# Holding the accumulation of f's leftover row behind the low part of its piece, in an encoder layer in split fp32

## The chip, the cores and the metric

The kernel runs on one core of one Trainium2 chip. The metric is the device time of one execution in microseconds (us), taken as the median of several runs. Besides that there is one execution recorded by the hardware profiler; its span runs from the first to the last instruction on the core.

## The reference

One encoder layer on x, 256 tokens of 2048 channels, all float32: a feed-forward half-step, a mixer, a second feed-forward half-step. The mixer is what matters here:

```python
u = _rms_norm(h, pre_g)
q, k, v, f, g = jnp.split(u @ w_in, SPLIT_POINTS, axis=-1)
q = _apply_axial_rope(_rms_norm(q.reshape(b, s, N_Q_HEADS, HEAD_DIM), q_norm_g), rope)
k = _apply_axial_rope(_rms_norm(k.reshape(b, s, N_KV_HEADS, HEAD_DIM), k_norm_g), rope)
...
y_attn = _blocked_gqa(q, k, v) @ w_attn_o
y_four = _fourier_mix(f) @ w_fourier
...
merged = gates[:, :, 0] * y_attn + gates[:, :, 1] * y_four
return h + _rms_norm(merged @ w_out, post_g)
```

`_fourier_mix` splits f (1024 channels) into 8 groups of 128 channels and takes the real part of the two-dimensional FFT over the 256 positions and the 128 channels of a group. g gives the gates through a sigmoid.

## The kernel before

**Numbers and pieces.** Every matrix product is done with fp32 values split in two: a high part (ScalarE copies the value into the matmul's reduced format, L101) and a low part (VectorE subtracts the high part from the value, L102). `split` does both and notes the two instructions as `latest["A"]` and `latest["V"]`. `mm3` makes three matmuls of one product: high by high (L106), weight's low (L107), activation's low (L108). A weight piece is 512 KB: two contraction rows of 128 by 512 columns (`piece`, L112). It is loaded by SyncE (L82) into one of 5 buffers `raw`, and its parts go into a ring of 6 high and 6 low buffers (`wring`), which become free when TensorE has used them.

**The stages.** First feed-forward (11 blocks of 512 hidden columns), then the mixer, then the second feed-forward. In the mixer a column block (`col_block`, L187) makes 512 columns of u @ w_in for both halves of the tokens: 16 contraction rows, 2 token tiles and 3 matmuls, 96 matmuls of 512 columns, with 8 weight pieces. `between` and `at` are lists of other work that is put among its matmuls. The order of the mixer around the change (L844 to L859) is v; gate 10, with the folding of the tokens and norm and rope of k among it; q's first block; gate 11, with norm and rope of q among it; gate 12, with the transposes of k; gate 13; then attention, with the Fourier parts among its first gate.

**The projection to f.** f is not made like q or k. The tokens come mirrored, so `fold_tokens` (L566) makes the even sum and the odd difference of the two token tiles, transposes them and splits them (`ueo`). The column of the transposed odd tile that has no partner is kept in `o0`, one value for each of the 2048 channels. The weight of f comes as 16 pieces, one for each contraction row, 512 KB each: `load_f` (L615) loads a piece into a buffer `fraw` (SyncE, L618) and then lets GpSimd's queue add the mirrored columns on the way from memory (252 KB, L613). The buffers come from the pool `chunk`, two tags of 3 buffers each, and pieces alternate between the tags: 6 buffers.

`fold_f` (L622) does one piece. It starts the load of the piece four further on, forms the differences of the mirrored columns on VectorE (L631, in place, held behind the latest low part by `tc.issue_after`), splits the piece (L101, L102), and adds 12 matmuls of 260 or 252 columns (names pe, accumulators `pfold`). Then follows the leftover row: z2, 128 x 520, gets the piece's first 260 columns of both halves times o0's value of this row, summed over the 16 pieces on VectorE (L642 for piece 0, L644 for the others; the profile names the tile zs). After the last piece `pfold` is split (fs), and `fourier_positions` (L660) reads zs and fs. `folds_at(4)` spreads four folds over a column block, one behind each of its rows 1, 5, 9 and 13: folds 0 to 3 lie in q's first block, 4 to 7 in gate 11, 8 to 11 in gate 12, 12 to 15 in gate 13.

**What sets the order.** Each engine works through its instructions in order. The order is made when the program is built: a scheduler places each instruction on its engine's queue by when its inputs, its buffers and its engine are free in the scheduler's plan, with the program's order as preference. So an instruction without further ties may stand well ahead of its place in the program. `with tc.issue_after(ins):` adds to every instruction in the block that runs on `ins`'s engine the tie that it comes after `ins` in that queue; it is no wait on another engine. One stretch (L303) is under a manual schedule for VectorE; the folds are not.

Of the kernel before, what the change touches and what calls it, by code (L numbers as in the profile page):

```python
# [15 lines left out]
ALU = mybir.AluOpType  # L16
# [38 lines left out]
def encoder_layer(  # L55
# [23 lines left out]
    V, A, T = nc.vector, nc.scalar, nc.tensor  # L79
# [18 lines left out]
    latest = {}  # L98

    def split(hi, lo, src):  # L100
        a = A.activation(hi, src, AF.Copy)  # L101
        v = V.tensor_tensor(out=lo, in0=src, in1=hi.bitcast(F32), op=ALU.subtract)  # L102
        latest["A"], latest["V"] = a.ins, v.ins

    def mm3(ps, lh, ll, rh, rl, first, last):
        T.matmul(ps, lh, rh, start=first, stop=False)  # L106
        T.matmul(ps, lh, rl, start=False, stop=False)  # L107
        return T.matmul(ps, ll, rh, start=False, stop=last)  # L108
# [415 lines left out]
    for nm, g in (("q", gq), ("k", gk)):  # L524
        gc = const.tile([P, NT, HD], F32, name="gc" + nm)
        gs = const.tile([P, NT, HD], F32, name="gs" + nm)
        for t in range(NT):
            V.tensor_tensor(out=gc[:, t, :], in0=rc[:, t, :], in1=g[:], op=ALU.mult)
            v = lambda a: a.rearrange("p (a h c) -> p a h c", a=2, h=2)
            for half in range(2):  # L530
                V.tensor_tensor(out=v(gs[:, t, :])[:, :, half, :], in0=v(rsn[:, t, :])[:, :, half, :],
                                in1=v(g[:])[:, :, 1 - half, :], op=ALU.mult)
# [30 lines left out]
    o0 = const.tile([P, KD], F32, name="o0")  # L563
# [44 lines left out]
    z2 = xpool.tile([P, 2, EW], F32, tag="xt", name="zs")  # L608
# [6 lines left out]
    def load_f(k):  # L615
        raw = chunk.tile([P, 2, NB], F32, tag=("ch_hi", "ch_lo")[k % 2], name="fraw")
        src = w_f[k].rearrange("p (b c) -> p b c", b=2)
        load(raw[:], src)  # L618
        add_on_the_way(raw[:, :, 0:OW], src[:, :, EW:NB])
        fraw[k] = raw  # L620

    def fold_f(k):  # L622

        if k == 0:
            pfold[0] = pmm.tile([P, NB], F32, tag="mm", name="pe")
            pfold[1] = ptr.tile([P, NB], F32, tag="tr", name="pe")
        if k + F_AHEAD < KD:
            load_f(k + F_AHEAD)
        raw = fraw.pop(k)
        with tc.issue_after(latest["V"]):  # L630
            V.scalar_tensor_tensor(out=raw[:, :, EW:NB], in0=raw[:, :, EW:NB], scalar=-2.0, in1=raw[:, :, 0:OW],  # L631
                                   op0=ALU.mult, op1=ALU.add)
        hi = wring.tile([P, 2, NB], F32R, tag="hi", name="whi")
        lo = wring.tile([P, 2, NB], F32R, tag="lo", name="wlo")
        split(hi[:], lo[:], raw[:])
        e, o = slice(0, EW), slice(EW, NB)
        for b in range(2):
            mm = mm3(pfold[b][:, e], ueo[0][0][:, k, :], ueo[0][1][:, k, :], hi[:, b, e], lo[:, b, e], k == 0, False)
            with tc.issue_after(mm.ins):
                mm3(pfold[b][:, o], ueo[1][0][:, k, :], ueo[1][1][:, k, :], hi[:, b, o], lo[:, b, o], False, k == KD - 1)  # L640
        if k == 0:
            V.tensor_scalar(out=z2[:], in0=raw[:, :, e], scalar1=o0[:, k:k + 1], scalar2=None, op0=ALU.mult)  # L642
        else:
            V.scalar_tensor_tensor(out=z2[:], in0=raw[:, :, e], scalar=o0[:, k:k + 1], in1=z2[:],  # L644
                                   op0=ALU.mult, op1=ALU.add)
        if k == KD - 1:
            fs.extend(chunk.tile([P, 2, NB], F32R, tag="ch_" + c, name="f" + c[0]) for c in ("hi", "lo"))
            for b in range(2):
                split(fs[0][:, b, :], fs[1][:, b, :], pfold[b][:])
# [3 lines left out]
    def folds_at(n):  # L653

        now = [folds.pop(0) for _ in range(n)]
        return [(1 + i * KD // n, lambda k=k: fold_f(k)) for i, k in enumerate(now)]
# [389 lines left out]
```

## Time and profile before

| | us |
|---|---|
| Median of 3 runs | 2110.78 (2110.67 to 2111.9) |
| The profiled execution | 2111.38 |
| Its span | 2109.6 |
| Mean granted TensorE clock | 0.992 of full speed |

How to read the lines that follow: a group or timeline line has the source line, the engine (PE is TensorE, PEld its weight loads, DVE VectorE, ACT ScalarE, POOL GpSimd, SP SyncE), the operation, and out<-in by the program's names. In a timeline the first two numbers are the start and the duration in us, and the bracket holds how long the engine had been idle and what ended that. A row of a stretch gives its length, then busy us with the number of instructions in brackets for PE, PEld, DVE, ACT and POOL, then the granted clock, the busy share of the DMA engines, and GB/s. A waits line reads: who, for whom, us in total, times, the longest. A matmul's own duration is longer than the distance to the next one, since matmuls are pipelined.

### The profile page before, as it was taken

What the parts mean: (1) busy time and instruction counts of PE and PEld (TensorE: products, weight loads), DVE (VectorE), ACT (ScalarE), POOL (GpSimd) and SP (SyncE); (2) the same over time, 40 slices, a digit from 0 to 9 for tenths busy, and PEclk for the clock granted to TensorE, in tenths of its full rate; (3) what the DMA queues carried; (4) which work ended last, traced back from release to release, by engine and by line L of the source; (5) the groups of instructions that cost most, each with busy time, mean ns of one, the idle gap of its engine ahead of it and who ended that gap; (6) DMA issues with size and microseconds to landing.
All of it is one profiled execution on the core that took longest, in us unless ns stands there. A gap on an engine that the chain in (4) does not pass through costs nothing.

```text
span 2109.6 us, 25216 instructions
## 1 busy us (share of the span) xinstructions
PE 2065.4 (98%) x9466; PEld 1711.0 (81%) x9466; DVE 1317.7 (62%) x1682; ACT 1008.5 (48%) x1336; POOL 50.8 (2%) x46
## 2 busy tenths in 40 slices
PE   9999999999999998799999999999999999999998
PEld 7888888888888877678888888878888888888886
DVE  6545555555555787567877886874555555555556
ACT  7444444444444555345676464554444444444443
POOL 0000000000000110100000000200000000000001
PEclk9999999999999999899999999999999999999999
DMA  8665655655655695664555657466555556555663
GB/s 317 221 214 191 189 191 189 193 191 189 191 189 196 204 286 175 166 180 156 182 178 180 209 174 265 163 195 212 191 191 190 190 191 195 190 189 189 192 191 108
DMA packets 117868, 411.11 MB, mean 195 GB/s; under 512 B 12873, under 2 KB 19025, under 8 KB 116337
## 3 DMA queue, kind: packets, MB, share of 16 engines
q1 hardware_dynamic: 113392, 405.36, 58.8%
q0 software_dynamic: 4352, 4.13, 1.3%
q8 instruction: 74, 1.21, 0.2%
q14 instruction: 50, 0.40, 0.1%
HBM read 405.25 MB, written 4.19 MB: 194 GB/s over the span
## 4 chain that ended last, share of the span: by engine, by line
PE 53%; DVE 3%; DMA 2%; issue 1%; ACT 0%; DVEq 0%; POOLq 0%; ACTq 0%
PE pc L106 10%; PE pc L108 10%; PE pc L107 10%; PE pr L108 6%; PE pr L107 6%; PE pr L106 6%; DMA fraw<-in_w_f 1%; DVE wlo L102 1%; PE pt L177 1%; DMA raw<-in_w_fo 1%; PE pt L761 0%; PE pf L108 0%; PE pf L106 0%; PE pf L107 0%; DVE h L390 0%
## 5 line engine op out<-in xcount | busy, mean ns | idle before, releaser
L102 DVE TENSOR_TENSOR wlo<-raw,whi 128x1024 fp32r<-128x1024 f32 (+1 forms) x711 | 866.4, 1221 | 669.6 <-ACT whi L101 668.0
L101 ACT ACTIVATE whi<-raw 128x1024 fp32r<-128x1024 f32 (+1 forms) x711 | 751.3, 1059 | 872.1 <-PE pc L108 525.0
L106 PE MATMUL pc<-whi,uh 128*128 128x512 f32 x1840 | 721.9, 392 | 1.5 <-ACT uh L485 1.5
L107 PE MATMUL pc<-wlo,uh 128*128 128x512 f32 x1840 | 719.6, 391 | 2.0 <-DVE wlo L102 2.0
L108 PE MATMUL pc<-whi,ul 128*128 128x512 f32 x1840 | 719.1, 391 | 2.0 <-DVE ul L102 2.0
L108 PEld LDWEIGHTS pc<-whi,ul 128*128 128x128 f32 x1840 | 347.0, 189 | 75.0 <-DVE ul L102 3.0
L106 PEld LDWEIGHTS pc<-whi,uh 128*128 128x128 f32 x1840 | 347.1, 189 | 73.8 <-ACT uh L485 3.3
L107 PEld LDWEIGHTS pc<-wlo,uh 128*128 128x128 f32 x1840 | 347.1, 189 | 73.8 <-DVE wlo L102 3.9
L106 PE MATMUL pr<-whi,hTh 128*128 128x512 f32 x688 | 269.5, 392 | 0.0
L108 PE MATMUL pr<-whi,hTl 128*128 128x512 f32 x688 | 267.9, 389 | 0.0
L107 PE MATMUL pr<-wlo,hTh 128*128 128x512 f32 x688 | 267.9, 389 | 0.0
L108 PEld LDWEIGHTS pr<-whi,hTl 128*128 128x128 f32 x688 | 129.2, 188 | 26.8
L106 PEld LDWEIGHTS pr<-whi,hTh 128*128 128x128 f32 x688 | 129.2, 188 | 26.1
L107 PEld LDWEIGHTS pr<-wlo,hTh 128*128 128x128 f32 x688 | 129.3, 188 | 26.0
L219 DVE TENSOR_TENSOR yf<-pr,yf 128x512 f32<-128x512 f32 (+1 forms) x82 | 55.1, 673 | 10.4 <-PE pr L108 9.7
L219 DVE TENSOR_TENSOR y<-pr,y 128x512 f32<-128x512 f32 x80 | 54.7, 685 | 4.5 <-PE pr L108 4.0
L106 PE MATMUL pr<-whi,oTh 128*128 128x512 f32 x128 | 50.3, 393 | 0.0
L108 PE MATMUL pr<-whi,oTl 128*128 128x512 f32 x128 | 50.0, 390 | 0.0
L107 PE MATMUL pr<-wlo,oTh 128*128 128x512 f32 x128 | 49.9, 390 | 0.0
L106 PE MATMUL pr<-whi,mTh 128*128 128x512 f32 x120 | 46.9, 391 | 0.0
L108 PE MATMUL pr<-whi,mTl 128*128 128x512 f32 x120 | 46.7, 389 | 0.0
L107 PE MATMUL pr<-wlo,mTh 128*128 128x512 f32 x120 | 46.7, 389 | 0.0
(300 smaller groups left out, 1378.0 us busy)
## 6 DMA issues: line engine op xcount, KB each, us to landing
raw<-in_f_up SPq DMA_DIRECT2D x176, 512.0 KB, 4.6
raw<-in_f_down SPq DMA_DIRECT2D x176, 512.0 KB, 4.5
raw<-in_f_gate SPq DMA_DIRECT2D x175, 512.0 KB, 4.4
raw<-in_w_in SPq DMA_DIRECT2D x112, 512.0 KB, 4.8
raw<-in_w_ao SPq DMA_DIRECT2D x32, 512.0 KB, 3.8
raw<-in_w_out SPq DMA_DIRECT2D x32, 512.0 KB, 4.2
fraw<-in_w_f SPq DMA_DIRECT2D x16, 512.0 KB, 6.0
raw<-in_w_fo SPq DMA_DIRECT2D x16, 512.0 KB, 4.3
```

The costliest lines, as they stand in the source:

```text
L101: a = A.activation(hi, src, AF.Copy)
L102: v = V.tensor_tensor(out=lo, in0=src, in1=hi.bitcast(F32), op=ALU.subtract)
L106: T.matmul(ps, lh, rh, start=first, stop=False)
L107: T.matmul(ps, lh, rl, start=False, stop=False)
L108: return T.matmul(ps, ll, rh, start=False, stop=last)
L177: T.transpose(pt[:, j, :], src[:, j * P:(j + 1) * P], ident[:])
L219: V.tensor_tensor(out=dst, in0=ps, in1=dst, op=ALU.add)
```

## The change

The two instructions that accumulate the leftover row are put under `tc.issue_after(latest["V"])`. At that place `latest["V"]` is the low part of the same piece, made by the `split` a few lines earlier. What is computed, and in which sums, stays as it was.

```diff
@@ -638,11 +638,12 @@
-        if k == 0:
-            V.tensor_scalar(out=z2[:], in0=raw[:, :, e], scalar1=o0[:, k:k + 1], scalar2=None, op0=ALU.mult)
-        else:
-            V.scalar_tensor_tensor(out=z2[:], in0=raw[:, :, e], scalar=o0[:, k:k + 1], in1=z2[:],
-                                   op0=ALU.mult, op1=ALU.add)
+        with tc.issue_after(latest["V"]):
+            if k == 0:
+                V.tensor_scalar(out=z2[:], in0=raw[:, :, e], scalar1=o0[:, k:k + 1], scalar2=None, op0=ALU.mult)
+            else:
+                V.scalar_tensor_tensor(out=z2[:], in0=raw[:, :, e], scalar=o0[:, k:k + 1], in1=z2[:],
+                                       op0=ALU.mult, op1=ALU.add)
```

## The prediction

> **What bounds the kernel now.** The page comes first: TensorE is busy nearly throughout, so the change can only pay where TensorE stands still. The two --windows rows below it (busy time in a stretch) compare all of the folding of f with its last part.
>
> ```profile
> PE 2065.4 (98%) x9466; PEld 1711.0 (81%) x9466; DVE 1317.7 (62%) x1682; ACT 1008.5 (48%) x1336; POOL 50.8 (2%) x46
> ```
> ```profile
> 814.97:955.23 140.26, 116.28 (x549) 97.65 (x548) 84.01 (x122) 58.52 (x83) 10.01 (x10) 0.90 0.60 172
> 927.71:955.23 27.52, 27.52 (x145) 23.65 (x144) 19.39 (x21) 14.65 (x15) 0.00 (x0) 1.00 0.56 182
> ```
>
> The stretch runs from fold 0's first matmul to fold 15's. TensorE works 116.28 of 140.26 us there, at a granted clock of 0.90. From fold 11 to fold 15 it works all of 27.52 us at clock 1.00: four cycles, so one cycle (four rows of a column block and one fold) takes 6.88 us when nothing is missing. Who TensorE waits for, and who VectorE waits for, is in the waits of 725 to 960 us (total, times, longest):
>
> ```profile
> PE pe L107 <- DVE wlo L102: 16.0, 6, 6.1
> PE pe L106 <- ACT q L546: 6.3, 1, 6.3
> PE pe L106 <- ACT whi L101: 1.6, 2, 1.2
> ```
> ```profile
> DVE zs L644 <- DMA fraw<-in_w_f: 36.4, 7, 7.1
> DVE zs L644 <- issue: 4.2, 1, 4.2
> ```
>
> TensorE lacks mostly the low part of a piece of f (16.0 us), which VectorE writes. VectorE itself stands 36.4 + 4.2 = 40.6 us in front of the accumulation of the leftover row, zs at L644, for a piece that has not landed. VectorE's timeline shows which piece:
>
> ```profile
> 820.49 0.76 DVE L644 SCALAR_TENSOR_TENSOR zs<-fraw,o,zs 128x520 f32<-128x520 f32 x1 [4.56 <-DMA fraw<-in_w_f]
> ...
> 854.00 2.35 DVE L102 TENSOR_TENSOR wlo<-raw,whi 128x1024 fp32r<-128x1024 f32 x2
> 856.27 0.68 DVE L631 SCALAR_TENSOR_TENSOR fraw<-fraw 128x504 f32<-128x504 f32 x1
> 864.03 0.76 DVE L644 SCALAR_TENSOR_TENSOR zs<-fraw,o,zs 128x520 f32<-128x520 f32 x1 [7.09 <-DMA fraw<-in_w_f]
> 864.71 1.22 DVE L102 TENSOR_TENSOR wlo<-fraw,whi 128x1024 fp32r<-128x1024 f32 x1
> ...
> 888.58 0.76 DVE L644 SCALAR_TENSOR_TENSOR zs<-fraw,o,zs 128x520 f32<-128x520 f32 x1 [5.74 <-DMA fraw<-in_w_f]
> 889.26 1.22 DVE L102 TENSOR_TENSOR wlo<-fraw,whi 128x1024 fp32r<-128x1024 f32 x1
> ...
> 937.89 2.35 DVE L102 TENSOR_TENSOR wlo<-raw,whi 128x1024 fp32r<-128x1024 f32 x2
> 940.16 0.67 DVE L631 SCALAR_TENSOR_TENSOR fraw<-fraw 128x504 f32<-128x504 f32 x1
> 942.01 1.23 DVE L102 TENSOR_TENSOR wlo<-fraw,whi 128x1024 fp32r<-128x1024 f32 x1 [1.18 <-ACT whi L101]
> ```
>
> Counting these instructions in order, the low part at 864.71 is that of piece 5, but the accumulation ahead of it, at 864.03, is that of piece 10. The accumulations stand about five pieces early in VectorE's queue, and the low part of piece 5, whose input is long there, waits 7.09 us behind a transfer of piece 10. That transfer can't be earlier, as SyncE and GpSimd show:
>
> ```profile
> 854.11 0.33 SPq L82 DMA_DIRECT2D fraw<-in_w_f  x1
> ...
> 865.96 0.33 SPq L82 DMA_DIRECT2D fraw<-in_w_f  x1
> ```
> ```profile
> 859.15 1.09 POOL L613 DMA_DIRECT2D fraw<-in_w_f  x1 [12.31 <-DMA fraw<-in_w_f]
> ```
>
> There are six buffers for f. Piece 10's load goes out at 854.11, when piece 4 has been read for the last time, GpSimd adds the mirrored half from 859.15, and the sum is there at 864.0. Piece 11's load goes out at 865.96, just behind the low part of piece 5 (864.71 + 1.22). So there is a ring: low part of k, load of k + 6, accumulation of k + 6, low part of k + 1. It is this ring that TensorE waits for.
>
> **The change, part by part.**
>
> *What it does to the queue.* The same 16 instructions stay; nothing is added on any engine and no DMA either. The accumulation of piece k goes behind the low part of piece k. Its input has landed by then, since the low part reads the same buffer, so it waits for no one, and the eight stalls, 40.6 us of VectorE, have no cause left. The ring above is cut.
>
> *What TensorE can win at most.* Fifteen cycles at 6.88 are 103.2 us. In the stretch lie also two groups of transposes of k:
>
> ```profile
> 913.67 0.60 PE L177 MATMUL pt<-ident,o 128*128 128x128 f32 x4
> 914.02 0.48 PE L106 MATMUL pc<-whi,uh 128*128 128x512 f32 x1
> ```
>
> They hold TensorE for 0.35 us each, 0.7 together. 140.26 - 103.2 - 0.7 = 36.3 us is lost in the stretch: 16.0 + 6.3 + 1.6 by these waits, and most of the rest by the slow clock after them:
>
> ```profile
> 908.05 0.39 PE L106 MATMUL pe<-whi,ueh 128*128 128x260 f32 x1 [1.23 <-ACT whi L101]
> 909.31 0.58 PE L107 MATMUL pe<-wlo,ueh 128*128 128x260 f32 x1 [0.87 <-DVE wlo L102]
> ...
> 912.26 0.63 PE L107 MATMUL pc<-wlo,uh 128*128 128x512 f32 x1
> 912.69 0.43 PE L108 MATMUL pc<-whi,ul 128*128 128x512 f32 x1
> ```
>
> Two matmuls of 512 columns start 0.43 us apart at 912.26 and 912.69; in the quick cycle above 24 such matmuls, and 12 of about half their columns, fit into 6.88 us, 0.23 for a long one. So from 909.31 to 912.69, 3.4 us, TensorE runs at about half pace, a loss of 1.7, and this after a gap of 0.87.
>
> *What becomes late next: VectorE.* I follow it to fold 7, where it is closest, because the norm and rope of q fall into folds 5 and 6. Its low part began at 889.26. Away go the six stalls before it, of which the first (4.56, at 820.49), the fifth (7.09) and the sixth (5.74) are shown; the six make 28.2 of the 40.6. Thirteen accumulations had run by then and only seven will have: 6 x 0.68 (from 864.03 to 864.71) = 4.1 away. A cover is lost too: between L631 and the low part VectorE must wait for ScalarE's high part, 1.18 at 942.01, and the accumulation stood in this gap in folds 2, 4, 5 and 7, and partly in 6: 4 x 1.18 + 0.6 = 5.3 comes back. 889.26 - 28.2 - 4.1 + 5.3 = 862.3, and 863.5 at its end. TensorE wants it at 814.97 + 7 x 6.88 = 863.1. So the two are level: 0.4 short. If none of the 4.1 is usable (it came from a time when VectorE may have to wait for others instead) and the cover is lost in all of the seven folds (8.3), it is 7.5 short. Between 0 and 7.5 I take 2.0, nearer to the worked-out 0.4, and add one slow stretch of 1.7: 3.7 us of the 36.3 stay.
>
> Both ends are kept for the range: nothing stays, or 7.5 with two slow stretches of 1.7, 10.9. In the steady cycles VectorE has room: from 937.89 to 942.01 and the low part's 1.2 is one cycle of about 5.3 us, 6.0 with an accumulation, against 6.88.
>
> *The rule on the clock.* The short gaps at 908.05 and 909.31, 1.23 and 0.87 us, are followed by half pace. The Trainium skill (TensorE: Matmul & The Clock Gate, Part 1: The HAM clock gate) says that the clock drops to half after an idle window of some 3.4 us and comes back after as much work. By that rule gaps of 2 us would cost only themselves, and as an estimate the time would be 1.7 us less than mine. The trace differs in this place, and I keep its 1.7.
>
> *The first wait.* The 6.3 us before fold 0's second half end with ScalarE's read of k in the norm. That read follows VectorE's chain for k (L156 to L167), whose steps stood behind the accumulation at 820.49, its stall of 4.56 and its 0.68. Without these 5.2 the wait is 1.1 us, with part of the 4.1 it is none; it lies inside the 2.0 above.
>
> *The loads.* The accumulation becomes the last reader of its buffer. SyncE issues load k + 6 when VectorE is through with piece k, so 0.68 later than behind the low part alone. Behind that load stand loads of w_in in SyncE's queue. Of these five buffers lie ahead, two pieces are used a cycle, so the lead is 2.5 cycles, 17 us, against these landing times (KB each, median us):
>
> ```profile
> raw<-in_w_in SPq DMA_DIRECT2D x15, 512.0 KB, 6.0
> fraw<-in_w_f POOLq DMA_DIRECT2D x3, 252.0 KB, 8.0
> fraw<-in_w_f SPq DMA_DIRECT2D x1, 512.0 KB, 6.9
> ```
>
> A delay of 0.68 is hidden, and piece k + 6 has six cycles, 41 us, for 6.9 + 8.0. If the cover were gone it would cost 0.68 ten times, 6.8. The last accumulation, beside fold 15, moves behind the low part of 15; its sum is read once the folds have ended, some 7 us later.
>
> **The sum.** The profiled execution took 2111.4 us, 1.8 more than its span of 2109.6, and 0.6 more than the median, 2110.8. 36.3 - 3.7 = 32.6 us go: 2078.8 for it, 2078.2 for a median. I say 2078.
>
> **The rivals.**
>
> *TensorE waits for nothing* during the folds: 2110.8 - 36.3 = 2074.5. For it: folds 11 to 15 already run so. Against it: VectorE is only level at fold 7.
>
> *VectorE takes over* from folds 5 to 9, with the far end above: 2110.8 - 36.3 + 10.9 = 2085.4.
>
> *Memory takes over.* A cycle moves 3 x 512 + 252 KB, 1.83 MB, which in 6.88 us is 266 GB/s (last column):
>
> ```profile
> 760.00:780.00 20.00, 20.00 (x90) 16.55 (x89) 16.33 (x40) 10.69 (x12) 2.19 (x2) 1.00 0.94 303
> 780.00:800.00 20.00, 20.00 (x102) 16.82 (x101) 17.21 (x23) 14.05 (x22) 1.08 (x1) 1.00 0.69 226
> ```
>
> At 226 GB/s a cycle would take 8.1 us, 1.2 more in each of the ten cycles that still load f: 2074.5 + 12 = 2086.5. Against it: 303 GB/s was reached with two of the adding transfers in it, and at 226 the engines were busy 0.69.
>
> *Slower.* The hold sets only how early the accumulation may stand. If it is planned far behind its low part, load k + 6 and the w_in loads behind it leave as late. From a delay of 17 - 6.0 = 11 us on this shows; at 2.5 cycles the lead is gone and each of ten loads costs its landing, 6.0: 2074.5 + 60 = 2134.5. Against it: L631 is held by the same means and stands right behind its low parts (854.00 and 856.27, 937.89 and 940.16).
>
> *The hold does nothing*, the accumulations stay early: 2110.8.
>
> **How the numbers follow.** The forecast (2075 to 2084) has 0.52, TensorE without a wait 0.13, VectorE 0.14, memory 0.10, no effect 0.05, slower 0.05; 0.01 lies between. The range from 2074 to 2092 takes in the first four and their bounds, 0.89 less some for their edges. Faster by over 0.2% (4.2 us, about what a measurement of this kernel can tell from no change) is 0.90, within it 0.05, slower 0.05.
>
> **What would show it.** In the new profile VectorE has no wait at L644 for a transfer; low part k is followed by accumulation k; folds start about 6.9 us apart, some of folds 5 to 9 up to 9; the clock is near 1.00 in the stretch, which ends some 33 us earlier. I am wrong if TensorE still waits over 8 us in it, if L631 or SyncE's queue waits for f in L644's place, or if time is lost elsewhere.

## The result and the profile after

The changed kernel takes 2076.95 us (2076.41 to 2078.75, 4 runs) against 2111.34 us (2110.67 to 2114.08, 4 runs) for the kernel before on the same chip: ratio 0.9836, 95% interval 0.9819 to 0.9853. The prediction was 2078, in a range of 2074 to 2092.

The profiled execution took 2076.99 us, its span is 2075.2. The rows of stretches below are of the kernel before and of the changed kernel: fold 0's first matmul to fold 15's, and from there to the end.

```profile
814.97:955.23 140.26, 116.28 (x549) 97.65 (x548) 84.01 (x122) 58.52 (x83) 10.01 (x10) 0.90 0.60 172
955.23:2109.60 1154.37, 1140.60 (x5297) 947.58 (x5295) 743.99 (x963) 567.31 (x783) 21.81 (x18) 1.00 0.58 188
```
```profile
814.60:920.42 105.82, 104.65 (x549) 89.38 (x548) 86.58 (x125) 58.49 (x83) 9.84 (x9) 1.00 0.78 228
920.42:2075.20 1154.78, 1140.75 (x5297) 947.45 (x5295) 743.80 (x963) 567.62 (x783) 21.87 (x18) 1.00 0.57 187
```

The whole gain lies in the first stretch: 140.26 - 105.82 = 34.4 us, as much as the span lost. Fold 0 starts at the same time but for 0.4 us, and the rest of the program is 0.4 longer. The clock in the stretch rose from 0.90 to 1.00 and memory's rate from 172 to 228 GB/s.

VectorE's and TensorE's waits of the changed kernel, 725 to 960 us, first VectorE's longest and then what TensorE waits for in the folds:

```profile
DVE wlo L102 <- ACT whi L101: 31.6, 27, 2.9
```
```profile
PE pe L106 <- ACT q L546: 1.2, 1, 1.2
```

The 40.6 us at the accumulation are gone; no wait of VectorE for a piece of f is left. TensorE's 16.0 us for the low part of f are gone from this list too, and of the 6.3 before fold 0's second half 1.2 are left. The timeline of VectorE shows the new order, and SyncE's the load behind it:

```profile
838.11 1.23 DVE L102 TENSOR_TENSOR wlo<-fraw,whi 128x1024 fp32r<-128x1024 f32 x1 [1.18 <-ACT whi L101]
839.26 0.75 DVE L645 SCALAR_TENSOR_TENSOR zs<-fraw,o,zs 128x520 f32<-128x520 f32 x1
839.93 2.35 DVE L102 TENSOR_TENSOR wlo<-raw,whi 128x1024 fp32r<-128x1024 f32 x2
842.20 0.68 DVE L631 SCALAR_TENSOR_TENSOR fraw<-fraw 128x504 f32<-128x504 f32 x1
844.05 1.23 DVE L102 TENSOR_TENSOR wlo<-fraw,whi 128x1024 fp32r<-128x1024 f32 x1 [1.18 <-ACT whi L101]
...
863.10 1.23 DVE L102 TENSOR_TENSOR wlo<-fraw,whi 128x1024 fp32r<-128x1024 f32 x1 [1.18 <-ACT whi L101]
864.24 0.75 DVE L645 SCALAR_TENSOR_TENSOR zs<-fraw,o,zs 128x520 f32<-128x520 f32 x1
```
```profile
865.07 0.33 SPq L82 DMA_DIRECT2D fraw<-in_w_f  x1
```

One cycle on VectorE is 844.05 - 838.11 = 5.94 us, with the accumulation in it. The low part at 863.10 is that of piece 7, the place where the prediction saw VectorE level with TensorE. The load at 865.07 is released by the accumulation of piece 7 (864.24 + 0.75). TensorE at the same place:

```profile
864.02 0.39 PE L108 MATMUL pc<-whi,ul 128*128 128x512 f32 x1
864.25 0.28 PE L106 MATMUL pe<-whi,ueh 128*128 128x260 f32 x1
864.38 0.39 PE L107 MATMUL pe<-wlo,ueh 128*128 128x260 f32 x1
```

The low part ends at 864.33 and its first matmul starts at 864.38, a little too late: fold 7 to fold 8 takes 7.03 us, 0.15 more than the 6.88 of the other cycles from fold 1 on. The two cycles that hold the transposes of k take 7.37.

### The profile page after: what moved, and what is told of

It is laid out like the page before. It is cut to its first block, busy times and chain, and to the rows that moved or that the text cites. A ratio compares the mean times of both kernels' runs of the same rounds, so it can differ in the third digit from the quotient of the medians.

```text
span 2075.2 us, 25220 instructions
## 1 busy us (share of the span) xinstructions
PE 2053.8 (99%) x9466; PEld 1702.6 (82%) x9466; DVE 1317.2 (63%) x1682; ACT 1008.1 (49%) x1336; POOL 50.9 (2%) x46
## 4 chain that ended last, share of the span: by engine, by line
PE 94%; DVE 4%; DMA 1%; ACT 1%; issue 0%; SPq 0%; DVEq 0%; ACTq 0%
PE pc L107 19%; PE pc L108 19%; PE pc L106 19%; PE pr L106 10%; PE pr L107 10%; PE pr L108 10%; PE pt L177 1%; DVE wlo L102 1%; DMA raw<-in_w_fo 1%; DVE h L390 0%; PE pe L106 0%; PE pe L108 0%; PE pe L107 0%; PE pt L762 0%; PE pf L108 0%
```

## The experiments

The theory: the accumulations stood up to six folds early in VectorE's queue and closed a ring (low part of k, load of k + 6, accumulation of k + 6, low part of k + 1); cutting the ring is the whole gain. Each experiment below is compared by its ratio to the kernel before on the same chip. The rivals: any early place costs its share; the place in the queue costs, and not the transfer; the accumulations cost VectorE's time.

**How early is too early.** Each fold's low part is kept, and the accumulation of piece k is held behind the low part of piece k - m (of piece 0 for the first ones). m = 0 is the changed kernel. From piece 6 on the kernel before is like m = 6, since no load of k goes out ahead of the low part of k - 6.

```diff
+        lows[k] = latest["V"]
...
+        with tc.issue_after(lows[max(0, k - m)]):
```

For m = 3, 4 and 5 the expectations were:

> The accumulation of piece k is held behind the low part of piece k - 3, so it may stand three folds early. Theory (a ring: low part of k, load of k + 6, accumulation of k + 6, low part of k + 1): the load of piece k + 3 went out three folds, some 20 us, before its accumulation comes up, against about 11.5 us from issue to the added half having landed; no wait, 2077 us (2075 to 2080). Rival (each fold of earliness costs its share of the 34 us between six folds early and none): half is lost, about 2094.

> The accumulation of piece k is held behind the low part of piece k - 4. Theory: round the ring it takes 11.5 us for load and adding, 0.7 for the accumulation and 5.3 from there to the next low part, 17.5 us, and with four folds early this is shared by three folds: 5.8 us a fold, under TensorE's 6.88; 2077 us (2076 to 2081). Rival (share of the earliness): about 2100.

> The accumulation of piece k is held behind the low part of piece k - 5. Theory: the 17.5 us round the ring are shared by two folds, 8.7 us a fold against 6.88, for the ten folds whose low part still releases a load: 18 us more than the changed kernel, 2095 us (2090 to 2101 with slow clock). Rival (share of the earliness): about 2106; a second rival (any lead below six folds is harmless, only the last step hurts): 2077.

Measured, each by the ratio to the kernel before: m = 3, 0.9832 [0.9815, 0.9848], 2077.87 us; m = 4, 0.9855 [0.9841, 0.987], 2082.53 us; m = 5, 0.9952 [0.9937, 0.9967], 2103.1 us. On this chip the kernel before took 2113.71, 2.4 more than beside the changed kernel. So three folds early cost nothing, four cost some 4 us by the ratio (0.9855 - 0.9836 = 0.0019 of 2111; against three folds on the same chip it is 4.7) and five some 24. For four no wait and 2077 were expected, for five 2095: both came out slower. Shares in proportion are out: they asked for about 2094 at three and 2100 at four. The waits of VectorE with m = 4 and with m = 5, 800 to 960 us:

```profile
DVE zs L646 <- DMA fraw<-in_w_f: 1.4, 1, 1.4
```
```profile
DVE zs L646 <- DMA fraw<-in_w_f: 22.9, 7, 4.1
```

With m = 3 there is no such row. With m = 4 there is one wait of 1.4 us, and folds 5, 6, 7 and 8 start 7.27, 8.65 and 8.13 us apart. So at four the wait for a transfer is not shown to be the whole loss: the next experiment, without any such wait, loses time at the same folds. With m = 5 VectorE waits some 3 us in seven folds. VectorE, SyncE and GpSimd of m = 5:

```profile
847.41 1.23 DVE L102 TENSOR_TENSOR wlo<-fraw,whi 128x1024 fp32r<-128x1024 f32 x1 [1.17 <-ACT whi L101]
851.61 0.76 DVE L646 SCALAR_TENSOR_TENSOR zs<-fraw,o,zs 128x520 f32<-128x520 f32 x1 [2.98 <-DMA fraw<-in_w_f]
854.56 0.68 DVE L631 SCALAR_TENSOR_TENSOR fraw<-fraw 128x504 f32<-128x504 f32 x1
856.41 1.23 DVE L102 TENSOR_TENSOR wlo<-fraw,whi 128x1024 fp32r<-128x1024 f32 x1 [1.18 <-ACT whi L101]
861.77 0.76 DVE L646 SCALAR_TENSOR_TENSOR zs<-fraw,o,zs 128x520 f32<-128x520 f32 x1 [4.05 <-DMA fraw<-in_w_f]
```
```profile
839.24 0.33 SPq L82 DMA_DIRECT2D fraw<-in_w_f  x1
...
848.67 0.33 SPq L82 DMA_DIRECT2D fraw<-in_w_f  x1
...
857.67 0.33 SPq L82 DMA_DIRECT2D fraw<-in_w_f  x1
```
```profile
844.51 1.09 POOL L613 DMA_DIRECT2D fraw<-in_w_f  x1 [8.36 <-DVE wlo L102]
...
854.88 1.09 POOL L613 DMA_DIRECT2D fraw<-in_w_f  x1 [9.29 <-DVE wlo L102]
```

The load issued at 839.24 is waited for until 851.61, 12.4 us (5.3 until GpSimd starts at 844.51, 7.1 from there), and that of 848.67 until 861.77, 13.1. The low part that follows the accumulation starts 856.41 - 851.61 = 4.8 us after it, takes 1.2, and releases the load of 857.67. So once round is 857.67 - 839.24 = 18.4 us, shared by two folds, 9.2 each; the expectation had 11.5 + 0.7 + 5.3 = 17.5. The ring was close to the right size. The ten cycles from fold 1 to fold 11, each taken from the first matmul with the low part, are 93.9 us: the first two, before VectorE has to wait, 7.0 and 7.2, fold 5 to 6, with norm and rope of q, 14.2, the seven others 9.4 on average. The 14.2 had been left out; with the 2.4 us by which the kernel before was slower on this chip it is enough for the 2 us by which 2103 lies above the range given.

The length of the ring is not fixed. In the kernel before one fold has it to itself, and the low parts of pieces 5 and 7 (864.71 and 889.26, shown in the prediction) lie 24.6 us apart, 12.3 a fold. There the differences were made before the wait (856.27), and the low part came right behind the accumulation.

**Early, but without a wait for a transfer.**

```diff
-            V.scalar_tensor_tensor(out=z2[:], in0=raw[:, :, e], scalar=o0[:, k:k + 1], in1=z2[:],
+            V.scalar_tensor_tensor(out=z2[:].rearrange("p b c -> p (b c)"), in0=ueo[0][0][:].rearrange("p k c -> p (k c)")[:, 0:2 * EW].bitcast(F32), ...
```

> The accumulations are not held at all, as in the kernel before, but read a slice of the transposed tokens instead of the piece of f, so that none waits for a transfer; the leftover row is then a wrong sum of the right size, and the buffers of f are released by the low part alone. Theory (the wait for the transfer is the cost, not the early place): the 16 instructions crowd into folds 0 to 3, where VectorE gets up to 7 us late and may cost 2 to 5 us, and all else is gone: 2077 to 2084. Rival (an accumulation ahead of the low parts costs by its place in the queue): 2105 or more.

Measured: 2081.67 us (2079.61 to 2082.29), ratio 0.9848 [0.9834, 0.9863]. The leftover row is not computed in this kernel. All 16 accumulations were done by 830.4 us, the last a dozen folds ahead of its low part, and by the ratios this costs some 2.5 us (0.9848 - 0.9836) against the changed kernel, with intervals that overlap. VectorE of this kernel:

```profile
824.48 0.76 DVE L644 SCALAR_TENSOR_TENSOR zs<-ueh,o,zs 128x520 f32<-128x520 f32 x1
825.29 0.75 DVE L644 SCALAR_TENSOR_TENSOR zs<-ueh,o,zs 128x520 f32<-128x520 f32 x1
825.96 1.22 DVE L102 TENSOR_TENSOR wlo<-fraw,whi 128x1024 fp32r<-128x1024 f32 x1
```

Three instructions one behind the other, the low part of piece 2 behind the accumulation of piece 13, and no idle time. It is the transfer that costs most, and not the place. What is lost was expected in folds 0 to 3 but lies mainly at folds 6 and 7, which take 8.53 and 8.13 us against 6.88 and 7.03 in the changed kernel. TensorE at fold 7:

```profile
866.19 0.39 PE L106 MATMUL pe<-whi,ueh 128*128 128x260 f32 x1 [0.90 <-ACT whi L101]
867.45 0.39 PE L107 MATMUL pe<-wlo,ueh 128*128 128x260 f32 x1 [0.87 <-DVE wlo L102]
```

No accumulation is left by then, and with m = 4 TensorE waits for the same two, 0.36 and 0.88 us at fold 7. What makes VectorE late there was not followed up.

**What the accumulations themselves cost.** Three kernels and the changed one, on one chip. In the first the accumulations are left out:

```diff
         if k == 0:
-            V.tensor_scalar(out=z2[:], in0=raw[:, :, e], scalar1=o0[:, k:k + 1], scalar2=None, op0=ALU.mult)
-        else:
-            V.scalar_tensor_tensor(out=z2[:], in0=raw[:, :, e], scalar=o0[:, k:k + 1], in1=z2[:],
-                                   op0=ALU.mult, op1=ALU.add)
+            V.memset(z2[:], 0.0)
```

In the second they stand behind the differences (d, L631) of the same piece, ahead of its split; in the third, at the same place, those of the piece before:

```diff
+        with tc.issue_after(d.ins):
+            if k == 0:
+                V.tensor_scalar(out=z2[:], in0=raw[:, :, e], scalar1=o0[:, k:k + 1], scalar2=None, op0=ALU.mult)
+            else:
...
```
```diff
+        if k:
+            with tc.issue_after(d.ins):
+                leftover(k - 1, held_raw[0])
```

> The 16 accumulations are left out and the leftover row is zero, so the Fourier branch lacks this term. Theory (what is left in the changed kernel is a wait of 1.2 us at fold 0 and under 1 us at folds 7 to 10): at most 1.5 us to win against the changed kernel, 2075.5 (2074 to 2077). Rival (the accumulations still cost VectorE time on the path, 16 x 0.68 = 11 us): 2066 to 2070.

> The accumulation of piece k is held behind the differences of the same piece (L631), ahead of the low part, where VectorE waits 1.18 us for ScalarE's high part. Theory: its input has landed there too, so no wait for a transfer, and it costs VectorE nothing: a fold on VectorE 5.3 us instead of 5.9; 2076.5 (2075 to 2078). Rival (it must be behind the low part): well over 2080.

> The accumulation of piece k - 1 is held behind the differences of piece k, so it fills the same gap one fold later, and the load of piece k + 5 is released some 5 us later. Theory: loads have a lead of 17 us in SyncE's queue, so the delay is hidden; VectorE's folds 0 and 1 are 0.7 shorter where the norm of k is late; 2076 (2075 to 2078). Rival (a later release starves the loads): 2085 or more.

> The changed kernel itself, beside the three others on one chip: 2077.

Measured: left out, 2078.01 us, ratio 0.9844 [0.983, 0.9857]; in the gap, 2078.2, 0.9843 [0.983, 0.9856]; one later, 2079.33, 0.9848 [0.9834, 0.9861]; the changed kernel, 2077.34, 0.9839 [0.9826, 0.9853]. All four are one time within their intervals, which reach some 3 us to either side. The first three lie 0.2 to 1.3 us above the ranges given, which promised a small gain; none came. So the accumulations cost nothing any more that these runs can show. In the gap they fit as thought; VectorE waits less for ScalarE's high part there, 0.51 against 1.18 us:

```profile
836.28 0.75 DVE L638 SCALAR_TENSOR_TENSOR zs<-fraw,o,zs 128x520 f32<-128x520 f32 x1
837.54 1.23 DVE L102 TENSOR_TENSOR wlo<-fraw,whi 128x1024 fp32r<-128x1024 f32 x1 [0.51 <-ACT whi L101]
```

It wins nothing, because in the folds TensorE waited for VectorE only at fold 7. And with the accumulations left out fold 7's wait is still there, even a little longer:

```profile
865.00 0.39 PE L107 MATMUL pe<-wlo,ueh 128*128 128x260 f32 x1 [0.53 <-DVE wlo L102]
```

One fold later releases each load some 5 us later, and the folds are not slower for it: 106.28 us from fold 0 to fold 15, against 106.1 for the changed kernel beside it. The lead in SyncE's queue is real.

**More work behind the low part.** The accumulation is followed by one more, or three more, times zero, so that the sums stay.

```diff
+            for _ in range(n):
+                V.scalar_tensor_tensor(out=z2[:], in0=raw[:, :, e], scalar=nil[:, 0:1], in1=z2[:], op0=ALU.mult, op1=ALU.add)
```

> The changed kernel with each accumulation followed by one more like it, times zero, so the sums stay as they were. Theory (VectorE is the next to be late, level with TensorE at fold 7): 8 x 0.68 = 5 us late there, and 6.6 us a fold plus the gates' 0.3 leave nothing to catch up: 2082 (2080 to 2086). Rival (VectorE has room): 2077.

> The changed kernel with each accumulation followed by three more like it, times zero. Theory: 8.0 us a fold on VectorE and 0.3 for the gates against 6.88 on TensorE; 16 x 2.04 = 32.6 us more work, less some 5 us of lead at the last fold: 25 to 28 us over the changed kernel, and up to 5 more for the slow clock, 2102 to 2110. Rival (VectorE has room, or the waits overlap with something else): under 2095.

Measured: one more, 2091.07 us, ratio 0.9899 [0.9882, 0.9915]; three more, 2105.51, 0.9968 [0.9956, 0.998]. The stretch of the folds in the two:

```profile
815.75:928.58 112.83, 107.62 (x550) 90.78 (x548) 94.36 (x137) 56.42 (x82) 10.02 (x10) 0.98 0.72 209
```
```profile
817.07:941.58 124.51, 113.08 (x550) 93.04 (x548) 112.30 (x167) 54.98 (x81) 10.92 (x10) 0.96 0.66 190
```

With three more VectorE is the bound: 112.30 of 124.51 us busy. The total lies in the range given, but only 18.7 us more than in the changed kernel lie in the folds, where 25 to 28 were expected, and 8.7 behind them, so that is in part luck. With one more the stretch is 7.0 us longer, where 5 were expected, and VectorE is late at folds 6 and 7; here is fold 6, and then the Fourier part:

```profile
860.53 0.38 PE L106 MATMUL pe<-whi,ueh 128*128 128x260 f32 x1 [2.03 <-ACT whi L101]
861.81 0.59 PE L107 MATMUL pe<-wlo,ueh 128*128 128x260 f32 x1 [0.89 <-DVE wlo L102]
...
938.89 0.33 PE L673 MATMUL pa<-odd,zh 128*126 128x130 f32 x1 [1.91 <-ACT zh L101]
941.63 0.47 PE L674 MATMUL pa<-odd,zl 128*126 128x130 f32 x1 [2.09 <-DVE zl L102]
```

The wait of 2.03 us for ScalarE's high part is VectorE's too: ScalarE made it from 859.42 on, and VectorE's differences ended at 859.35. But the time rose by 13 us (0.9899 - 0.9836 of 2111), not 5, and is outside the range given. Of the 13.2 us by which the spans differ 1.2 lie ahead of the folds and some 5 behind them, in the Fourier part, where TensorE waits 1.91 and 2.09 us at 938.89 and 941.63 against one wait of 1.11 in the changed kernel. These were not in the estimate. The accumulations themselves were over at 929.7, so the wait for zh is not one for their sum. ScalarE and then VectorE show what stood ahead of zh and zl:

```profile
937.24 1.29 ACT L797 ACTIVATE mB<-z 128x512 f32<-128x512 f32 x2 [1.12 <-DVE z L796]
938.43 0.40 ACT L101 ACTIVATE zh<-zs 128x260 fp32r<-128x260 f32 x1
```
```profile
940.55 0.69 DVE L813 TENSOR_TENSOR raw<-raw 128x512 f32<-128x512 f32 x1 [1.55 <-DMA raw<-in_w_fo]
941.15 0.42 DVE L102 TENSOR_TENSOR zl<-zs,zh 128x260 fp32r<-128x260 f32 x1
```

zh stood behind the gate, which waited for VectorE, and zl behind an instruction that waited 1.55 us for a transfer (0.83 in the changed kernel): the pattern of the leftover row once more, in another place. What makes VectorE late there was not followed up.

## Why the prediction was right

**The ring** is the mechanism that the prediction named, and the tests bear it out: cutting it at the accumulation removes all eight waits; closing it again a little looser (five folds) brings back 22.9 of 40.6 us; giving the accumulation an input that needs no transfer takes it away without moving the instruction back. What an earliness of four folds costs is not explained by it alone.

**The ceiling.** 36.3 us was the most that TensorE could win; 34.4 came. After the change the stretch is 15 x 6.88 = 103.2 and 2.6 more: 1.5 in the cycle of fold 0, of which 1.17 is TensorE's wait, 0.15 at fold 7, and 0.49 for each of the two transposes. The prediction had 0.35 for each of these, 0.7, and 3.7 for all waiting.

**What stays.** The wait before fold 0's second half was put at 1.1 us or none; it is 1.17. The low part of piece 7 was to begin at 862.3; it begins at 863.10. VectorE's cycle was put at 6.0; it is 5.94. The shortfall at fold 7 was put at 0.4 worked out and 2.0 taken; it is about 0.15. That this came so near is in part luck: the low part is 0.8 later than worked out, and TensorE 1.1 later than the 863.1 given for it, as its first wait had not been counted on the way to fold 7.

**Where it was off.** Two places. The 1.7 us for one slow stretch was too much: among the folds no stretch at half pace came after the change. And the account of fold 7, in which each accumulation counts 0.68 us of VectorE's time, does not hold, though the result came near: without any accumulation the low part should be ready some 5 us earlier, but TensorE still waits 0.53 us there. In that stretch, folds 5 and 6, VectorE and ScalarE hand norm and rope of q to and fro, and both kernels come out of it level with TensorE. That the hand-overs are what sets it was not tried by itself. VectorE has room for one accumulation in a fold; with two it comes late where norm and rope of q are, while the last four cycles take 6.88 us each but for one of 7.26.

**The other rivals.** Memory moved 228 GB/s over the whole stretch, but TensorE waited for no transfer there, so it was not the bound. The hold acts as wanted, each accumulation right behind its low part, so neither the late nor the idle hold came true; a release 5 us later still cost nothing in the folds.

## What to carry to other kernels

An instruction that is ready in the plan but not in fact, and stands early in a queue that is worked through in order, makes everything behind it wait for its transfer. Look for an engine that idles for a DMA while the next instruction's input has long been there. Then look whether the blocked work also releases the next transfer: that closes a ring, and its length divided by the folds that share it gives the time of one step. The length has to be read in the order at hand: it was 18.4 us for two folds with m = 5 and 12.3 for one in the kernel before. What cutting the ring is worth is read on the engine that is the bound: TensorE lost 36.3 us, slow clock included, and 34.4 came back. An instruction need not be moved all the way back: three folds early, out of six, was harmless here.

## What was not expected of the hardware

TensorE's pace halved after gaps that are short, and not each time. In the kernel with m = 5:

```profile
847.43 0.39 PE L106 MATMUL pe<-whi,ueh 128*128 128x260 f32 x1 [1.14 <-ACT whi L101]
848.69 0.39 PE L107 MATMUL pe<-wlo,ueh 128*128 128x260 f32 x1 [0.88 <-DVE wlo L102]
...
850.82 0.63 PE L106 MATMUL pc<-whi,uh 128*128 128x512 f32 x1
851.25 0.63 PE L107 MATMUL pc<-wlo,uh 128*128 128x512 f32 x1
```

After gaps of 1.14 and 0.88 us the long matmuls start 0.43 us apart instead of 0.23. In the same kernel 1.39 and 0.87 us at 917.72 and 918.98 were followed by the full pace, as was the single 1.17 in the changed kernel. Two executions of the changed kernel differ even at one and the same single gap, in the Fourier part behind the folds. Here is the one taken beside the kernel without accumulations:

```profile
929.47 0.33 PE L669 MATMUL pa<-odd,zl 128*126 128x130 f32 x1 [1.10 <-DVE zl L102]
...
932.16 0.63 PE L106 MATMUL pc<-whi,uh 128*128 128x512 f32 x1
932.59 0.63 PE L107 MATMUL pc<-wlo,uh 128*128 128x512 f32 x1
```

The granted clock from 931 to 935 us is 0.57. In the execution of the section on the result the gap is 1.11 us, at 930.38; the long matmuls behind it start 0.23 us apart, and the clock from 932 to 936 is 1.00. So gaps of 1 to 2 us in all sometimes cost a stretch at half pace and sometimes not. What decides it is not shown here. The Trainium skill (TensorE: Matmul & The Clock Gate, Part 1: The HAM clock gate) names an idle window of some 3.4 us. These traces show the drop with less idle time than that.
